# Turning new keys and values into token rows: VectorE 32x32 block transposes and 128 B stores in place of TensorE transposes

## The chip, the cores and the metric

The kernel runs on one core of a Trainium2 chip. The metric is device time in microseconds (us) of one execution. A core has a matrix engine (TensorE; PE in the profile, its weight loads PEld), a vector engine (VectorE, DVE), a scalar engine (ScalarE, ACT), GpSimd (POOL) and a sync engine (SP) that here issues nearly all DMAs. Each engine runs its own instructions in the order in which the program lists them; semaphores join the engines. SBUF is the on-chip memory with 128 partitions, PSUM holds the results of TensorE, DRAM is off-chip.

## The reference, cut to what matters

One inference step of a hybrid layer: 1040 prompt tokens (16 learned meta tokens, then 1024 real ones) and 32 sample tokens (8 requests of 4), all of width 2048. They go through one input projection into eight stick-breaking attention heads of width 128, four gated-linear-attention heads and their gates, and then through one output projection. Besides the layer's result the step returns the new keys and values of the eight heads, as token rows:

```python
def step(...):
    (q, k, v), sg, (gq, gk, gv, gf), gg = branch_inputs(h, w_in[l], w_alpha[l], b_alpha[l])
    o_sb = sb_prompt(q, k, v, sb_bias[l])
    ...
    k_p.append(k)      # (1, 1, 1040, 8, 128) after the stack
    v_p.append(v)
    ...
    k_s.append(k)      # (1, 8, 4, 8, 128)
    v_s.append(v)
```

In `new_k_prompt[0, 0, token, head, :]` the 128 numbers of one token and head are 512 contiguous bytes; the next token of the same head lies 4096 bytes further.

## The kernel before, in words

**Projection.** `inproj` makes one 128-column slice of the input projection for all 1072 tokens, with the result transposed: 128 output columns on the partitions, tokens along the free dimension. Every fp32 operand is split in a high and a low part, so each product is three matmuls (lines 289 to 291). The loop runs over eight weight chunks of 256 rows; in each over three groups of tokens with an accumulator each; in each over two row blocks. That makes 18 matmuls per chunk and 144 per slice. `weight_chunk` loads a chunk (`wr`), ACT casts it (`wh`, line 184) and DVE subtracts (`wl`, line 185). Each of the three tiles has three buffers, and weight work is urgent for the scheduler. After the last chunk `evac` copies each accumulator out.

**Token groups.** `CHUNKS` are 384, 384 and 304 tokens. Values and keys use `SCHUNKS` instead: 378, 378 and 316, which are multiples of `KT` = 126, since the attention's key tiles hold 126 keys and one carry column.

**Heads.** `head(h)` makes the values (`ev_v`), the keys (`ev_k`) and the queries of a head, and then spawns its attention. So PE works through slices V, K, Q of head 0, V, K, Q of head 1 and so on, and the attention of a head is woven into the slices of the next. The table of the profile below gives the three slices of one head.

**What happens to a value or key group.** ACT copies the accumulator to a staging tile `raw` (128 head columns x tokens). `split_k` splits keys into high and low parts in the layout of the key tiles (ACT line 601, DVE line 602). `tok_out` turns the group into token rows: three TensorE transposes (line 457) into one PSUM tile, copies by ACT into a staging tile `st` (lines 459 to 462), and stores on the SP queue of 512 B per token (lines 465 to 468). `load_v` (lines 478, 480) later reads the values back from the output in DRAM, as token rows, for the attention.

**The other work in the same time.** `z_feed` scores the sample queries against the paged key cache on DVE: for each of 512 pages a load of 64 KB (`kp`, line 342) and four multiply-and-accumulate instructions (`jk`, line 384). A page is taken every two beats, a beat being a third of a weight chunk, and loads run six pages ahead. `attend_tile` is a chain PE `z` (505 to 507), DVE 511, ACT 512 and 513, DVE 514, ACT and DVE split (490, 491), PE `z` again (526, 527), ACT 531, split (490, 491), PE `O` (539 to 541). The stages of one tile are set `yield 2`, `D1` = 4 and `D2` = 6 beats apart.

**Order.** The program emits instructions through a `Weaver`, whose generators are continued after a number of beats, and a scheduler then fixes each engine's order when the kernel is built. At run time every engine, and SP's DMA issue, keeps that order.

Of the kernel before, what the change touches and what calls it, by code (L numbers as in the profile page):

```python
# [10 lines left out]
F32 = mybir.dt.float32  # L11
# [71 lines left out]
def hybrid_step(ctx: ExitStack, tc: tile.TileContext, x_prompt, x_sample, cache_k, cache_v, state_gla,  # L83
# [3 lines left out]
    nc = tc.nc  # L87
# [21 lines left out]
    def stage(nm, dt=F32):  # L109
        return stg.tile([P, 384], dt, tag="stg", name=nm)  # L110
# [79 lines left out]
    with tc.tile_pool(name="xp", bufs=2) as xp, tc.tile_pool(name="xps", bufs=5, space=PSUM) as xps:  # L190
# [57 lines left out]
        for c, (lo, hi) in enumerate(CHUNKS):  # L248
            n = hi - lo
            for k in range(NK):  # L250
# [14 lines left out]
                    load_x(5)  # L265
                if (c, k) in NORMS:
                    norm_x(NORMS[c, k])
            lo, hi = SCHUNKS[c]
            o_ = first[c][:, :hi - lo]
            for k in range(NK):  # L270
                wh, wl = (t[:, k % 2, :] for t in wchunks[k // 2])
# [4 lines left out]
                for i in (6, 7, 8):  # L276
                    load_x(i)

    def inproj(c0, evac, lo0, nm, chunks=CHUNKS):

        acc = [accp.tile([P, 512], F32, tag="acc", name=f"acc_{nm}_{c}") for c in range(3)]
        for kk in range(NK // 2):
            wh, wl = weight_chunk(w_in[0], kk, c0, f"{nm}_{kk}")
            for c, (lo, hi) in enumerate(chunks):
                lo = max(lo, lo0)
                n = hi - lo
                for k2 in range(2):
                    k = 2 * kk + k2
                    mm(acc[c][:, :n], wh[:, k2, :], hh[k][:, lo:hi], start=(k == 0), stop=False)  # L289
                    mm(acc[c][:, :n], wh[:, k2, :], hl[k][:, lo:hi], start=False, stop=False)  # L290
# [153 lines left out]
    with tc.tile_pool(name="sp", bufs=1) as sp, tc.tile_pool(name="sps", bufs=1, space=PSUM) as sps:  # L444
# [1 line left out]
        bias0 = sp.tile([P, HEADS], F32, name="bias0")  # L446
        vec.tensor_copy(bias0[:], biasb[:])
        pool.memset(bias0[0:1, :], -1e30)
        def tok_out(raw, c, lo, hi, h, outp, outs_, nm):

            yield 6
            os_ = outs_[0].rearrange("b t h d -> (b t) h d")
            ps = sps.tile([P, 512], F32, tag="z", bufs=4, name=f"tk_{nm}_{c}")
            st = stage(f"st_{nm}_{c}")
            for i in range(3):
                r = min(KT, hi - lo - i * KT)
                nc.tensor.transpose(ps[:r, i * P:(i + 1) * P], raw[:, i * KT:i * KT + r], ident[:])
# [12 lines left out]
        def load_v(h, V):  # L470

# [105 lines left out]
            heads_ready.append(h)  # L577

        def head(h):
            def ev_v(c, ps, lo, hi):  # L580
                raw = stage(f"vraw{h}_{c}")
                act.copy(raw[:, :hi - lo], ps)
                W.spawn(tok_out(raw, c, lo, hi, h, new_v_prompt, new_v_sample, f"v{h}"))
            if h:
                inproj(C_SV + h * P, ev_v, 0, f"v{h}", SCHUNKS)
            else:
                for c, (lo, hi) in enumerate(SCHUNKS):
# [6 lines left out]
            ks = sp.tile([P, NSMP], F32, tag="ks", name=f"ks{h}")  # L594

            def split_k(raw, c, lo, hi):
                for i0, n, w in ((0, 3, KT),) if c < 2 else ((0, 2, KT), (2, 1, 32)):
                    d = [t[:, (3 * c + i0) * P:(3 * c + i0 + n) * P] if w == KT else t[:, 8 * P:KW] for t in kt]
                    d = [t.rearrange("p (a x) -> p a x", a=n)[:, :, 1:w + 1] for t in d]
                    r = raw[:, i0 * KT:i0 * KT + n * w].rearrange("p (a x) -> p a x", a=n)  # L600
                    act.copy(d[0], r)
                    vec.tensor_tensor(d[1], r, d[0].bitcast(F32), ALU.subtract)
# [12 lines left out]
            qsm = sp.tile([P, NSMP], F32, tag="qsm", name=f"qsm{h}")  # L615

# [924 lines left out]
```

## Time and profile before

| | |
|---|---|
| three runs, median (lowest to highest) | 2123.5 us (2121.63 to 2123.98) |
| span of the profiled execution, its own time | 2126.0 us, 2.5 us over the median |
| granted TensorE clock, mean | 0.993 |
| slices V, K, Q of head 2, start to start | 309.4, 339.3, 373.1 and 402.3 us: 29.9, 33.8 and 29.2 us |
| heads' slices on PE | from the first key slice at 73.6 us to the first gate slice at 796.6 us |
| transposes of `tok_out` | from 80.4 us (values of head 0) to 753.9 us (keys of head 7) |

Reading the profile: the page gives each engine's busy time over the span, then 40 slices of the span, then the chain of waits that ends last, then groups of instructions, `out<-in`, with count, busy time and mean duration. The duration of a matmul covers its way through the array, so successive ones overlap, and the time that one adds to PE is better read from start to start. On DVE too the recorded durations of neighbours overlap by some 0.08 us. The windows view gives the busy time of each engine between two moments.

### The profile page before, as it was taken

How to read it: one execution, taken by the hardware profiler on the slowest of the kernel's cores; microseconds unless marked ns; L12 is line 12 of the kernel's file. 1: busy time of each engine (PE TensorE's matmuls, PEld its weight loads, DVE VectorE, ACT ScalarE, POOL GpSimd, SP SyncE). 2: the span in 40 equal slices, each digit the busy share in tenths (PEclk: the TensorE clock that was granted, in tenths of full speed). 3: DMA queues.
4: the chain of work that ended last, by engine and by line, in shares of the span. 5: the costliest groups of instructions: out<-in, count | busy, mean ns of one | idle time of the engine just before them, and what ended most of it. 6: DMA issues, size and time to landing. Idle time of an engine off the chain costs nothing.

```text
span 2126.0 us, 43346 instructions
## 1 busy us (share of the span) xinstructions
PE 2062.8 (97%) x12546; PEld 1872.1 (88%) x12546; DVE 1573.4 (74%) x6592; ACT 995.7 (47%) x2536; POOL 81.8 (4%) x298
## 2 busy tenths in 40 slices
PE   5999999999999999999999999999999999999997
PEld 5999999999999989999898998998888897777765
DVE  6368888889888889898798898978544446453575
ACT  7345556565555646434435335353444335342332
POOL 0000000100001000100000000000000000000000
PEclk9999999999999999999999999999999999999999
DMA  6234443544444354554343444335777665452484
GB/s 198 72 99 127 129 127 103 142 127 113 136 130 121 109 138 118 158 137 116 113 128 109 132 122 128 96 86 151 239 225 241 223 192 185 136 153 75 129 285 171
DMA packets 380442, 304.02 MB, mean 143 GB/s; under 512 B 50410, under 2 KB 320682, under 8 KB 380202
## 3 DMA queue, kind: packets, MB, share of 16 engines
q1 hardware_dynamic: 378010, 300.97, 49.0%
q8 instruction: 99, 1.62, 0.3%
q14 instruction: 141, 1.16, 0.2%
q10 hardware_dynamic: 2192, 0.27, 0.1%
HBM read 243.39 MB, written 57.72 MB: 142 GB/s over the span
## 4 chain that ended last, share of the span: by engine, by line
PE 82%; DVE 7%; DMA 6%; ACT 2%; issue 2%; SPq 0%; POOL 0%; ACTq 0%; DVEq 0%; POOLq 0%
PE acc_g L289 4%; PE acc_g L291 4%; PE acc_g L290 4%; PE b L1450 4%; PE b L1451 4%; PE b L1452 4%; PE acc_k L289 3%; PE acc_k L290 3%; PE acc_k L291 3%; PE acc_q L289 3%; PE acc_q L290 3%; PE acc_q L291 3%; PE acc_v L289 3%; PE acc_gv L289 3%; PE acc_gv L291 3%; PE acc_gv L290 3%
## 5 line engine op out<-in xcount | busy, mean ns | idle before, releaser
L384 DVE SCALAR_TENSOR_TENSOR jk<-kp,qb 128x128 f32<-128x128 f32 x2048 | 591.0, 289 | 39.7 <-DMA qb<-qsd 2.3
L289 PE MATMUL acc_g<-hT,wh_g 128*128 128x368 f32 (+2 forms) x768 | 251.3, 327 | 1.3 <-ACT gx L438 1.2
L291 PE MATMUL acc_g<-hT,wl_g 128*128 128x368 f32 (+2 forms) x768 | 248.0, 323 | 0.0
L290 PE MATMUL acc_g<-hT,wh_g 128*128 128x368 f32 (+2 forms) x768 | 247.6, 322 | 0.0
L1450 PE MATMUL b<-ring,f 128*128 128x512 f32 x416 | 166.7, 402 | 6.6 <-ACT gx L438 3.7
L1314 DVE TENSOR_TENSOR ring<-wr,ring 128x512 fp32r<-128x512 f32 x104 | 70.7, 690 | 134.8 <-ACT ring L1313 134.3
L384 DVE DVE_READ_ACCUMULATOR jk<-kp,qb 128x1 f32 x2048 | 166.4, 81 | 0.0
L1451 PE MATMUL b<-ring,f 128*128 128x512 f32 x416 | 163.5, 393 | 0.8 <-DVE ring L1314 0.7
L1452 PE MATMUL b<-ring,f 128*128 128x512 f32 x416 | 163.2, 392 | 0.0
L289 PEld LDWEIGHTS acc_g<-hT,wh_g 128*128 128x128 f32 x768 | 144.7, 188 | 13.1 <-issue 7.3
L291 PEld LDWEIGHTS acc_g<-hT,wl_g 128*128 128x128 f32 x768 | 144.6, 188 | 2.0 <-issue 2.0
L290 PEld LDWEIGHTS acc_g<-hT,wh_g 128*128 128x128 f32 x768 | 144.7, 188 | 0.7
L1313 ACT CAST ring<-wr 128x512 fp32r<-128x512 f32 x104 | 64.4, 622 | 163.0 <-DMA wr<-in_w_out_dram 72.9
L289 PE MATMUL acc_gv<-hT,wh_gv 128*128 128x384 f32 (+1 forms) x384 | 129.2, 337 | 0.0
L289 PE MATMUL acc_k<-hT,wh_k 128*128 128x378 f32 (+1 forms) x384 | 127.6, 332 | 0.0
L290 PE MATMUL acc_k<-hT,wh_k 128*128 128x378 f32 (+1 forms) x384 | 125.4, 326 | 0.0
L289 PE MATMUL acc_q<-hT,wh_q 128*128 128x368 f32 (+2 forms) x384 | 125.3, 326 | 0.0
L291 PE MATMUL acc_gv<-hT,wl_gv 128*128 128x384 f32 (+1 forms) x384 | 125.3, 326 | 0.0
L291 PE MATMUL acc_k<-hT,wl_k 128*128 128x378 f32 (+1 forms) x384 | 125.2, 326 | 0.0
L290 PE MATMUL acc_gv<-hT,wh_gv 128*128 128x384 f32 (+1 forms) x384 | 124.7, 325 | 0.0
L290 PE MATMUL acc_q<-hT,wh_q 128*128 128x368 f32 (+2 forms) x384 | 123.6, 322 | 0.0
L291 PE MATMUL acc_q<-hT,wl_q 128*128 128x368 f32 (+2 forms) x384 | 123.5, 322 | 0.0
(427 smaller groups left out, 5403.5 us busy)
## 6 DMA issues: line engine op xcount, KB each, us to landing
kp<-in_cache_k_dram SPq DMA_DIRECT2D x512, 64.0 KB
vr<-in_cache_v_dram SPq DMA_DIRECT2D x64, 512.0 KB
tf<-in_w_out_dram SPq DMA_DIRECT2D x64, 256.0 KB
qb<-qsd SPq DMA_DIRECT2D x64, 256.0 KB
td<-tf SPq DMA_DIRECT2D x64, 256.0 KB
wr_g<-in_w_in_dram SPq DMA_DIRECT2D x128, 128.0 KB
wr<-td SPq DMA_DIRECT2D x64, 256.0 KB
wr<-in_w_out_dram SPq DMA_DIRECT2D x48, 256.0 KB
```

The costliest lines, as they stand in the source:

```text
L289: mm(acc[c][:, :n], wh[:, k2, :], hh[k][:, lo:hi], start=(k == 0), stop=False)
L290: mm(acc[c][:, :n], wh[:, k2, :], hl[k][:, lo:hi], start=False, stop=False)
L291: W.mark = mm(acc[c][:, :n], wl[:, k2, :], hh[k][:, lo:hi], start=False, stop=(k == NK - 1)).ins
L384: ins = vec.scalar_tensor_tensor(jk[:], kp[:], 1.0, qbs[h, b][:, t, :], ALU.mult, ALU.mult, accum_out=zt[:, t, NPG - 1 - i:NPG - i])
L1313: act.copy(wh, r)
L1314: vec.tensor_tensor(wl, r, wh.bitcast(F32), ALU.subtract)
L1450: mm(bk[:], ah, wh, start=first and k == 0, stop=False, skip_group_check=True)
L1451: mm(bk[:], ah, wl, start=False, stop=False, skip_group_check=True)
L1452: mm(bk[:], al, wh, start=False, stop=last and k == 7, skip_group_check=True)
```

## The change

`tok_out` no longer uses PE, PSUM or ACT. DVE transposes each 32x32 block of the staged group in place of a full transpose, into one tile `st` of 128 x 1088 for the whole slice (`vst` for values, `kst` for keys; both share one buffer). In that tile, partition 32i + r holds, for every block j, the 32 head columns 32i to 32i + 31 of token 32j + r. After the third group four DMAs, one for each i, store the tokens 0 to 1023 of the head: each moves 32 x 32 runs of 32 numbers, 128 B. The last 16 prompt tokens and the sample tokens have blocks of their own and DMAs of their own; those of the keys' last 16 tokens are kept in `tails` for all heads and stored by `last_keys` after head 7. Since 378 is no multiple of 32, values and keys go back to `CHUNKS`, and `split_k` cuts the groups where the 126-key tiles begin: eight pieces per head where there were four.

```diff
-SCHUNKS = [(0, 3 * KT), (3 * KT, 6 * KT), (6 * KT, T)]
...
-        def tok_out(raw, c, lo, hi, h, outp, outs_, nm):
-            yield 6
-            os_ = outs_[0].rearrange("b t h d -> (b t) h d")
-            ps = sps.tile([P, 512], F32, tag="z", bufs=4, name=f"tk_{nm}_{c}")
-            st = stage(f"st_{nm}_{c}")
-            for i in range(3):
-                r = min(KT, hi - lo - i * KT)
-                nc.tensor.transpose(ps[:r, i * P:(i + 1) * P], raw[:, i * KT:i * KT + r], ident[:])
-            if c < 2:
-                act.copy(st[:KT], ps[:KT, :384])
-            else:
-                act.copy(st[:KT, :256], ps[:KT, :256])
-                act.copy(st[:64, 256:], ps[:64, 256:384])
-            sv = st[:].rearrange("p (a d) -> p a d", d=P)
-            nt = 3 if c < 2 else 2
-            nc.sync.dma_start(outp[0, 0, lo:lo + nt * KT, h, :].rearrange("(a p) d -> p a d", p=KT), sv[:KT, :nt])
-            if c == 2:
-                nc.sync.dma_start(outp[0, 0, 8 * KT:REAL, h, :], sv[:32, 2, :])
-                nc.sync.dma_start(os_[:, h, :], sv[32:64, 2, :])
+        tails = sp.tile([P, HEADS, 32], F32, name="tails")
+        def tok_out(raw, c, lo, hi, h, st, outp, outs_, keep):
+            yield 2
+            w = 384 if c < 2 else 256
+            vec.transpose(st[:, lo:lo + w], raw[:, :w])
             if c < 2:
+                return
+            last = tails[:, h, :] if keep else st[:, SEQ:SEQ + 32]
+            vec.transpose(last, raw[:, SEQ - lo:SEQ + 32 - lo])
+            vec.transpose(st[:, SEQ + 32:], raw[:, REAL - lo:T - lo])
+            yield 1
+            for i in range(4):
+                dst = outp[0, 0, 0:SEQ, h, 32 * i:32 * i + 32].rearrange("(j r) c -> r j c", r=32)
+                nc.sync.dma_start(dst, st[32 * i:32 * i + 32, 0:SEQ].rearrange("r (j c) -> r j c", c=32))
+            if not keep:
+                for i in range(4):
+                    nc.sync.dma_start(outp[0, 0, SEQ:REAL, h, 32 * i:32 * i + 32], st[32 * i:32 * i + META, SEQ:SEQ + 32])
+            a = outs_[0].rearrange("b t h d -> (b t) h d")[:, h, :]
+            nc.sync.dma_start(bass.AP(tensor=a.tensor, offset=a.offset, ap=[[32, 4], [HEADS * P, NSMP], [1, 32]]),
+                              st[:, SEQ + 32:])
+        def last_keys():
+            for i in range(4):
+                nc.sync.dma_start(new_k_prompt[0, 0, SEQ:REAL, :, 32 * i:32 * i + 32], tails[32 * i:32 * i + META])
...
+            vst = sp.tile([P, SEQ + 64], F32, tag="st", name=f"vst{h}")
...
-                inproj(C_SV + h * P, ev_v, 0, f"v{h}", SCHUNKS)
+                inproj(C_SV + h * P, ev_v, 0, f"v{h}")
...
             def split_k(raw, c, lo, hi):
-                for i0, n, w in ((0, 3, KT),) if c < 2 else ((0, 2, KT), (2, 1, 32)):
...
+                t0, e = lo, min(hi, REAL)
+                while t0 < e:
+                    i, x = divmod(t0, KT)
+                    n = (e - t0) // KT if x == 0 else 0
+                    w = KT if n else min(KT - x, e - t0)
+                    n = max(n, 1)
...
                     act.copy(d[0], r)
                     vec.tensor_tensor(d[1], r, d[0].bitcast(F32), ALU.subtract)
+                    t0 += n * w
...
+            kst = sp.tile([P, SEQ + 64], F32, tag="st", name=f"kst{h}")
...
-                W.spawn(tok_out(raw, c, lo, hi, h, new_k_prompt, new_k_sample, f"k{h}"))
-            inproj(C_SK + h * P, ev_k, 0, f"k{h}", SCHUNKS)
+                W.spawn(tok_out(raw, c, lo, hi, h, kst, new_k_prompt, new_k_sample, True))
+                if c == 2 and h == HEADS - 1:
+                    W.spawn(last_keys(), 4)
+            inproj(C_SK + h * P, ev_k, 0, f"k{h}")
```

More of the change, by code (lines that the diff above doesn't have):

```diff
@@ L277, in hybrid_step, with inproj @@
                     load_x(i)
-    def inproj(c0, evac, lo0, nm, chunks=CHUNKS):
+    def inproj(c0, evac, lo0, nm):
         acc = [accp.tile([P, 512], F32, tag="acc", name=f"acc_{nm}_{c}") for c in range(3)]
@@ L283, in inproj @@
             wh, wl = weight_chunk(w_in[0], kk, c0, f"{nm}_{kk}")
-            for c, (lo, hi) in enumerate(chunks):
+            for c, (lo, hi) in enumerate(CHUNKS):
                 lo = max(lo, lo0)
@@ L470, in load_v @@
+        def last_keys():
+            for i in range(4):
+                nc.sync.dma_start(new_k_prompt[0, 0, SEQ:REAL, :, 32 * i:32 * i + 32], tails[32 * i:32 * i + META])
+            return
+            yield
         def load_v(h, V):
@@ L582, in ev_v @@
                 act.copy(raw[:, :hi - lo], ps)
-                W.spawn(tok_out(raw, c, lo, hi, h, new_v_prompt, new_v_sample, f"v{h}"))
+                W.spawn(tok_out(raw, c, lo, hi, h, vst, new_v_prompt, new_v_sample, False))
             if h:
-                inproj(C_SV + h * P, ev_v, 0, f"v{h}", SCHUNKS)
+                inproj(C_SV + h * P, ev_v, 0, f"v{h}")
             else:
-                for c, (lo, hi) in enumerate(SCHUNKS):
+                for c, (lo, hi) in enumerate(CHUNKS):
                     with urgent():
@@ L596, in split_k @@
             def split_k(raw, c, lo, hi):
[L597 to L600 removed]
+                t0, e = lo, min(hi, REAL)
[4 more added lines that the diff above has]
+                    n = max(n, 1)
+                    if n > 1:
+                        d = [t[:, i * P:(i + n) * P].rearrange("p (a x) -> p a x", a=n)[:, :, 1:w + 1] for t in kt]
+                        r = raw[:, t0 - lo:t0 - lo + n * w].rearrange("p (a x) -> p a x", a=n)
+                    else:
+                        d = [t[:, i * P + 1 + x:i * P + 1 + x + w] for t in kt]
+                        r = raw[:, t0 - lo:t0 - lo + w]
                     act.copy(d[0], r)
                     vec.tensor_tensor(d[1], r, d[0].bitcast(F32), ALU.subtract)
+                    t0 += n * w
                 if c == 2:
```

1 line of the change is left out of this document (removed).

## The prediction, made before the result was known

> **What bounds the kernel now.** I read the page's totals and slices first, then the chain of waits, then the windows of one head.
>
> ```profile
> span 2126.0 us, 43346 instructions
> PE 2062.8 (97%) x12546; PEld 1872.1 (88%) x12546; DVE 1573.4 (74%) x6592; ACT 995.7 (47%) x2536; POOL 81.8 (4%) x298
> PE   5999999999999999999999999999999999999997
> DVE  6368888889888889898798898978544446453575
> PE 82%; DVE 7%; DMA 6%; ACT 2%; issue 2%; SPq 0%; POOL 0%; ACTq 0%; DVEq 0%; POOLq 0%
> ```
>
> PE is busy in every slice and makes 82% of the chain that ends last. The DVE row stands at 8 or 9 tenths just where the heads run (slices 3 to 15). So work taken from PE counts there in full, and work given to DVE goes to the engine with the least room. The windows view of head 2 says how little; its lines are the slices V, K and Q.
>
> ```profile
> 309.40:339.30 29.90, 29.90 (x185) 28.63 (x185) 25.76 (x131) 15.41 (x45) 3.15 (x9) 1.00 0.48 136
> 339.30:373.10 33.80, 33.80 (x200) 31.95 (x200) 30.58 (x137) 21.42 (x51) 1.25 (x5) 1.00 0.40 103
> 373.10:402.30 29.20, 29.20 (x184) 28.59 (x183) 24.11 (x119) 16.98 (x44) 3.10 (x13) 1.00 0.58 160
> ```
>
> The columns are length, then busy time of PE, PEld, DVE, ACT and POOL, the granted clock, the DMA share and GB/s. PE has no idle time in 92.9 us. DVE has 29.90 - 25.76 = 4.1 us in V, 3.2 in K and 5.1 in Q. The clock is 1.00, so nothing is to be won there.
>
> **What PE loses.** The first two rows are from PE's timeline and give starts, the last two from the chain of waits.
>
> ```profile
> 160.54 0.49 PE L457 MATMUL tk_v<-ident,vraw 128*126 128x128 f32 x3
> 160.79 0.39 PE L289 MATMUL acc_k<-hT,wh_k 128*128 128x316 f32 x1
> ...
> 344.77 0.33 PE tk_v L457 x3
> 377.99 0.33 PE tk_k L457 x3
> ```
>
> Three transposes take 0.25 us from their start to the next matmul's, and 0.33 us on the chain. There are 16 tensors (values and keys of eight heads) of three such sets: 48 sets, 12.0 to 15.8 us. I take 0.28 us and 13.4 us, 1.7 us per head; none of it is hidden, as PE has no idle time.
>
> The groups become 384, 384, 304 in place of 378, 378, 316, the same 1072 columns. Keys (before) and linear-attention values (already in the other groups) show the price:
>
> ```profile
> L290 PE MATMUL acc_gv<-hT,wh_gv 128*128 128x384 f32 x256 | 86.2, 337 | 0.0
> L290 PE MATMUL acc_k<-hT,wh_k 128*128 128x378 f32 x256 | 86.1, 336 | 0.0
> L290 PE MATMUL acc_k<-hT,wh_k 128*128 128x316 f32 x128 | 39.3, 307 | 0.0
> L290 PE MATMUL acc_gv<-hT,wh_gv 128*128 128x304 f32 x128 | 38.5, 301 | 0.0
> ```
>
> Twice +1 and once -6 ns, 48 times in each of 16 tensors, would be -3 us; that is within the scatter of such means, so I take 0 with 3 us to either side.
>
> **What ACT loses** are four evacuations per tensor, and it gains eight small split pieces in place of four per head. ACT is busy 21.42 of 33.80 us at most, so I count nothing; it can only answer DVE sooner.
>
> **What DVE gains.** No 32x32 transpose stands in the trace. The nearest rows are two-operand passes of the same widths; a one-operand pass bounds them from below.
>
> ```profile
> L429 DVE TENSOR_TENSOR gs<-gs,gx 128x384 f32<-128x384 f32 x16 | 8.8, 552 | 0.0
> L185 DVE TENSOR_TENSOR wl_gv<-wr_gv,wh_gv 128x256 fp32r<-128x256 f32 x64 | 27.0, 422 | 1.5 <-ACT wh_gv L184 1.2
> L602 DVE TENSOR_TENSOR k<-kraw,k 128x32 fp32r<-128x32 f32 x8 | 1.5, 192 | 1.8 <-ACT k L601 1.8
> L236 DVE TENSOR_SCALAR x<-x,r_x 128x1024 f32<-128x1024 f32 x16 | 11.4, 750 | 0.3
> ```
>
> Per tensor: 552 + 552 + 422 + 2 x 192 ns = 1.91 us, 3.8 per head. The lower end is half of it (750 ns for 1024 columns is 281 for 384); the upper end is twice it, should a block have to be filled before it is emptied. I take the middle, since both operations move one fp32 element per column. Four more split pieces per head add at most 4 x 0.16 us (192 ns less the 32 columns). Neighbours overlap, as two rows of DVE's timeline show (start, duration):
>
> ```profile
> 357.71 0.42 DVE L185 TENSOR_TENSOR wl_k<-wr_k,wh_k 128x256 fp32r<-128x256 f32 x1
> 358.05 0.28 DVE L384 SCALAR_TENSOR_TENSOR jk<-kp,qb 128x128 f32<-128x128 f32 x1
> ```
>
> That is 0.08 us, 14 times a head: 3.8 + 0.6 - 1.1 = 3.3 us.
>
> There is a second load. In the built kernel's SP order, the stores of values stand between weight loads, and between two page loads (`kp`) now stand five weight loads and nine stores, where before it was one or two weight loads. DVE's order follows: of 49 `jk` in a V slice, 38 remain in head 4 and 31 in head 5; the others move into K and Q. The row is the K window for `jk` alone:
>
> ```profile
> 339.30:373.10 33.80, 14.74 (x101) 0.00 (x0) 1.00 0.40 103
> ```
>
> 101 instructions are some 50 `jk` with their accumulator reads: 0.29 us each, so 11 to 18 of them are 3.2 to 5.2 us.
>
> K and Q together: DVE 30.58 + 24.11 + 3.3 + 3.2 to 5.2 = 61.2 to 63.2 us, against 63.0 - 1.7 = 61.3 us of PE. To this come DVE's waits in these two windows that PE's lead doesn't cause:
>
> ```profile
> DVE X L514 <- ACT X L513: 2.2, 5, 1.0
> DVE lo_a L491 <- ACT hi_a L490: 1.1, 2, 0.7
> DVE V L484 <- ACT V L483: 1.1, 1, 1.1
> ```
>
> With these 4.4 us DVE is 4.3 to 6.3 us late by the end of Q. V takes that back: 25.76 less 3.2 to 5.2 of 29.9 us.
>
> **What is late next.** A chunk lasts 33.8 / 8 = 4.2 us in K and 3.65 in Q. `wl` is made two chunks ahead (three buffers), 7.3 to 8.4 us, which holds the lag. The attention has six beats, two chunks, between `z` and the split that PE needs, and its own chain takes part of that:
>
> ```profile
> L511 DVE TENSOR_SCALAR X<-z,bias 127x512 f32<-127x512 f32 x48 | 35.8, 746 | 3.4 <-PE z L507 3.3
> L512 ACT ACTIVATE X<-X 127x512 f32<-127x512 f32 x48 | 30.3, 630 | 45.0 <-DVE X L511 44.8
> L513 ACT ACTIVATE X<-X 127x512 f32<-127x512 f32 x48 | 30.1, 628 | 0.3
> L514 DVE SCALAR_TENSOR_TENSOR X<-z,bias,X 127x512 f32<-127x512 f32 x48 | 35.9, 748 | 8.0 <-ACT X L513 8.0
> L490 ACT CAST hi_s<-X 127x512 fp32r<-127x512 f32 x48 | 29.6, 616 | 0.3
> L491 DVE TENSOR_TENSOR lo_s<-X,hi_s 127x512 fp32r<-127x512 f32 x48 | 32.9, 685 | 0.7 <-ACT hi_s L490 0.7
> ```
>
> These sum to 4.05 us, which leaves 3.3 to 4.4 us for a lag of 4.3 to 6.3. Not every tile meets the worst of it, so I take 0.7 us of PE per head in the seven slice triples with attention beside them: 5 us. The bounds are 0 and the rival below.
>
> **Stores, SP and the new waits.** Small packets are in the trace: one load of 2048 runs of 64 B, here with its neighbours in a window of 1.6 us, and its issue on SP with the one behind it.
>
> ```profile
> DMA packets 380442, 304.02 MB, mean 143 GB/s; under 512 B 50410, under 2 KB 320682, under 8 KB 380202
> q1 hardware_dynamic: 378010, 300.97, 49.0%
> ...
> DMA packets 2204, 0.16 MB, mean 97 GB/s; under 512 B 2203, under 2 KB 2203, under 8 KB 2203
> q1 hardware_dynamic: 2203, 0.15, 94.0%
> ...
> 756.93 0.41 SPq L302 DMA_DIRECT2D war<-in_w_in_dram  x1
> 757.43 1.25 SPq L389 DMA_DIRECT2D zd<-zt  x1
> ```
>
> A packet there costs 1.6 us x 16 x 0.94 / 2203 = 11 ns of an engine; over the whole span it is 2126 x 16 x 0.49 / 378010 = 44 ns. A new store of 1024 runs thus takes 0.7 to 2.8 us on the 16 engines, and a tensor's four 2.8 to 11. They are spread over four chunks (15 us) with the queue 40 to 58% busy, so weight loads, issued some three chunks before the cast, stay covered. I count 0. [...]
>
> [...]
>
> `kst` shares its buffer with `vst`, so DVE's first key transpose waits for the value stores; behind it stand `wl` and the attention. SP has the last of these stores ahead of the third query chunk's load, which waits for the split of the last key chunk, and DVE reaches the transpose two chunks (7.3 us) later: hidden, unless a store train takes over 7 us more. `load_v` moves behind the next head's values on SP, and the last `O` of each head keeps its slice in PE's order: nothing.
>
> **Sum.** -13.4 + 0 + 5 = -8.4 us. The profiled span of 2126.0 is 2.5 us over the median of the runs, so it becomes 2117.6, and the median 2123.5 becomes 2115. With no lag and 15.8 + 3 us won it is 2105.
>
> **Rivals.**
>
> - *DVE becomes the bound in K and Q.* At the upper price of the transposes 3.8 us per head come on top, so the lag is 8.1 to 10.1 us, some 5.2 past what the attention holds, in seven triples 37 us: 2123.5 - 13.4 + 37 = 2147. It decides from the point where the lag exceeds 5.7 us (13.4 / 7 paid per head), which is about 0.72 us for a 384-column transpose. For it: 30.58 of 33.80 us busy. Against it: V's idle time refills the lead each head, and waits on ACT shrink when DVE is late. [...]
> - *The small stores hold up the loads.* At 100 ns a packet a store takes 6.4 us, a train 25.6 us where 14.8 are there; past the weights' lead of 8.4 us remain 2.4 us, in 15 trains 36: 2123.5 - 13.4 + 36 = 2146. Against it: 11 and 44 ns above.
> - *The gain is given back.* Lag and longer groups (+3) eat 10 to 17 of the 13.4 us: 2120 to 2127. For it: PE never idles in a head now, and any new wait shows at once.
>
> **How the numbers follow.** Forecast 0.50 (its own range 2105 to 2119), DVE as the bound 0.30, gain given back 0.12, stores 0.08. The measurement tells 0.2%, 4.2 us, from no change. Faster: 0.47 of the forecast's half and 0.01 = 0.48; same: 0.03 + 0.10 = 0.13; slower: 0.30 + 0.08 + 0.01 = 0.39. The range goes from 2106 to 2146 and so takes in most of the slower cases.
>
> **What would show it.** Right: no row for line 457's transposes on PE; PE busy time in the heads unchanged per us but the first gate slice starting some 8 us earlier than 796.6; block transposes of 0.55 us for 384 columns; DVE idle near zero in K and Q, over 6 us in V; waits of PE on `hi_s`, `lo_s` of a few us. Wrong: transposes of 0.8 us and more, PE waiting on DVE for over 15 us in the heads, weight casts waiting for DMA, SP issues of several us at the stores, or heads as long as before.

## The result and the profile after

The changed kernel takes 2199.3 us (median of five runs, 2196.4 to 2200.0) where the kernel before took 2121.6 beside it: ratio 1.0357, 95% interval 1.0346 to 1.0368. It is slower by 3.6%, where a gain had been forecast, and above the predicted range. These lines of its page answer to those of before.

```profile
span 2194.6 us, 42807 instructions
...
PE 2079.6 (95%) x12402; PEld 1872.1 (85%) x12402; DVE 1593.1 (73%) x6704; ACT 983.8 (45%) x2504; POOL 84.1 (4%) x298
...
PE   5999999899989887999999999999999999999997
...
DVE  6477878796878787989889798887644437453475
...
PE 53%; DVE 11%; DMA 8%; ACT 3%; issue 3%; SPq 2%; POOL 0%; DVEq 0%; POOLq 0%; ACTq 0%
```

PE's row has 8s and a 7 where it had only 9s, all in the heads; its share of the chain falls from 82% to 53%. 144 matmuls are gone and PE's busy time has nevertheless grown by 16.8 us. DVE does not look like a new bound: its row is no fuller than before.

The windows view from the first key slice to the first gate slice (length; busy time of PE, PEld, DVE, ACT, POOL; clock; DMA share; GB/s) says what was lost where. First before, then after, then a run shown below in which the four stores are one transfer of 512 B runs (e2).

```profile
73.60:796.60 723.00, 719.96 (x4388) 686.36 (x4386) 594.11 (x2767) 399.39 (x1025) 55.82 (x198) 1.00 0.45 123
```

```profile
73.00:870.20 797.20, 738.10 (x4243) 686.91 (x4242) 613.30 (x2873) 388.42 (x993) 57.41 (x198) 0.96 0.43 110
```

```profile
72.00:776.80 704.80, 701.07 (x4245) 665.79 (x4243) 608.59 (x2879) 383.17 (x993) 56.80 (x198) 1.00 0.46 126
```

The whole loss lies here: the first gate slice starts 73.6 us later than before, and what lies behind it is no longer than before (1324.4 us for 1329.4). Against e2, which has the same instructions on PE, DVE and ACT, the heads are 92.4 us longer. PE stands idle 797.2 - 738.1 = 59.1 us in place of 3.7 (55.4 more), and its 4243 matmuls take 738.1 us in place of 701.1 (37.0 more) at a mean clock of 0.96.

**One stall followed back.** These are rows of the timelines of PE, ACT and SP in a query slice of the changed kernel (start, duration; in brackets the idle time ahead and what ended it).

```profile
606.75 0.33 PE L287 MATMUL acc_q<-hT,wh_q 128*128 128x384 f32 x1
612.09 0.49 PE L545 MATMUL O<-hi_a,V 127*128 127x150 f32 x1 [5.01 <-ACT hi_a L496]
```

```profile
593.66 0.59 ACT L550 COPY ost<-O 128x512 f32<-128x512 f32 x1 [2.09 <-DVE lo_a L497]
...
610.89 0.39 ACT L537 ACTIVATE Y<-z,bias 127x150 f32<-127x150 f32 x1 [4.67 <-DMA od<-ost]
...
611.72 0.32 ACT L496 CAST hi_a<-Y 127x150 fp32r<-127x150 f32 x1 [0.28 <-POOL Y L539]
```

```profile
605.39 0.39 SPq L179 DMA_DIRECT2D wr_q<-in_w_in_dram  x1
606.57 0.34 SPq L340 DMA_DIRECT2D kp<-in_cache_k_dram  x1
606.95 0.43 SPq L403 DMA_DIRECT2D tf<-in_w_out_dram  x1
607.43 0.43 SPq L551 DMA_DIRECT2D od<-ost  x1
```

PE stands 5.01 us for `hi_a`; that waits for `Y`, and `Y` for a buffer that it shares with `ost`, the attention output of another tile. `ost` stood ready at 594.25 us, but SP issued its store at 607.43, 13.2 us later: in the built order fourteen other transfers stand between. Three of them are weight loads that wait for VectorE to free a buffer (0.6, 1.5 and 1.4 us by SP's waits); most of the rest is the time that SP takes to issue them, six page loads with the reads of their page numbers above all (some 1.1 us each on SP's timeline). Over all 16 such stores the time from the end of the copy to the issue has a median of 13.1 us, against 0.5 before.

Where SP itself waits has changed with the order (waits view of SP from 80 to 860 us, before and after; lines 180 and 179 are weight loads, 342 and 340 page loads):

```profile
SPq L342 <- DVE jk L384: 75.3, 116, 2.7
SPq L180 <- DVE jk L384: 69.2, 102, 4.9
```

```profile
SPq L179 <- DVE jk L382: 132.5, 92, 4.6
...
SPq L340 <- DVE jk L382: 6.7, 11, 1.4
```

Summed over all such rows of the heads, SP waits 124 us at weight loads and 88 at page loads before, 248 and 10 after. A page, an output or a re-read that stands behind such a weight load waits along with it. The waits view of 73 to 870 us (total, times, longest) names the other transfers that came late in the same way: pages for the score products, and values read back from DRAM.

```profile
DVE jk L382 <- DMA kp<-in_cache_k_dram: 55.7, 38, 4.4
```

```profile
ACT Y L537 <- DMA od<-ost: 47.7, 11, 8.4
ACT V L489 <- DMA vr<-out_dram: 23.5, 14, 6.2
```

**What a stall costs PE.** The windows view, microsecond by microsecond behind that stall:

```profile
612.38:613.40 1.02, 1.02 (x6) 1.02 (x5) 0.98 (x3) 0.13 (x1) 0.00 (x0) 0.50 0.41 116
...
616.40:617.40 1.00, 1.00 (x5) 1.00 (x4) 0.76 (x5) 0.93 (x3) 0.28 (x1) 0.50 0.00 0
617.40:618.40 1.00, 1.00 (x7) 1.00 (x7) 1.00 (x5) 0.23 (x1) 0.00 (x0) 0.88 0.00 1
```

Behind the 5.01 us of idleness the granted clock stands at 0.50 until 617.6 us, for 5.5 us after PE has resumed. Matmuls of 368 columns start 0.31 us apart in this stretch (from 616.48 us), 0.17 us apart ahead of the stall (from 605.75 us). So this stall is paid once as idle time and again at the lower clock.

The heads of the changed kernel have twelve stretches at 0.50. This is the windows view's sum over them (length; busy time of the engines):

```profile
sum 64.86, PE 50.05 PEld 45.84 DVE 49.71 ACT 27.76 POOL 7.81; mean PE 4.17 PEld 3.82 DVE 4.14 ACT 2.31 POOL 0.65
```

PE starts 168 matmuls in these stretches. At the 701.07 / 4245 = 0.165 us that one adds in e2 they would take 28 us. So some 22 of the 37.0 us are the half clock, by this estimate; the other 15 came at a clock of 1.00, and no run isolates their cause.

**What had been feared.** The group of VectorE's transposes of values (from the view of the tile; minimum, median, maximum in ns), and the DMA view of 201.0 to 204.0 us, in which one key store was issued at 201.05:

```profile
L453 DVE STREAM_TRANSPOSE vst<-vraw x24: 432/570/578, 72.5 to 763.4; 128x384 f32<-128x384 f32 x16, 128x256 f32<-128x256 f32 x8
L457 DVE STREAM_TRANSPOSE vst<-vraw x8: 166/201/209, 74.2 to 764.0; 128x32 f32<-128x32 f32 x8
```

```profile
DMA  0000000012453699999999999988100000000000
...
DMA packets 1313, 0.27 MB, mean 90 GB/s; under 512 B 1056, under 2 KB 1312, under 8 KB 1312
```

A transpose of 384 columns takes 0.57 us, and 1024 runs of 128 B are through within 2.2 us of their issue (by the DMA records they are moved in the last 1.0 us of it). By the updates of the DMAs' semaphores a store of the four lands 2.7 us after its issue (median), a weight load 2.4 before and 2.3 to 2.4 after, a page 2.2 and 2.0. Neither weight loads nor pages have become slower; they are issued late.

### The profile page after: what moved, and what is told of

Its sections match the earlier page's. It is cut to its first block, busy times and chain, and to the rows that moved or that the text cites. A ratio compares the mean times of both kernels' runs of the same rounds, so it can differ in the third digit from the quotient of the medians.

```text
span 2194.6 us, 42807 instructions
## 1 busy us (share of the span) xinstructions
PE 2079.6 (95%) x12402; PEld 1872.1 (85%) x12402; DVE 1593.1 (73%) x6704; ACT 983.8 (45%) x2504; POOL 84.1 (4%) x298
## 4 chain that ended last, share of the span: by engine, by line
PE 53%; DVE 11%; DMA 8%; ACT 3%; issue 3%; SPq 2%; POOL 0%; DVEq 0%; POOLq 0%; ACTq 0%
PE acc_g L287 4%; PE acc_g L289 4%; PE acc_g L288 4%; DVE jk L382 4%; PE b L1471 4%; PE b L1472 4%; PE b L1473 4%; PE acc_gv L287 2%; PE acc_gv L288 2%; PE acc_gv L289 2%; PE acc_gq L289 1%; PE dO L1112 1%; PE acc_gq L288 1%; PE acc_gq L287 1%; DMA kp<-in_cache_k_dram 1%
## 5 line engine op out<-in xcount | busy, mean ns | idle before, releaser
L287 PE MATMUL acc_q<-hT,wh_q 128*128 128x368 f32 (+2 forms) x384 | 127.8, 333 | 1.8 <-ACT kraw L629 1.8
L287 PE MATMUL acc_k<-hT,wh_k 128*128 128x384 f32 (+1 forms) x384 | 126.4, 329 | 0.0
L288 PE MATMUL acc_q<-hT,wh_q 128*128 128x368 f32 (+2 forms) x384 | 126.3, 329 | 0.0
L288 PE MATMUL acc_k<-hT,wh_k 128*128 128x384 f32 (+1 forms) x384 | 124.8, 325 | 0.0
L289 PE MATMUL acc_k<-hT,wl_k 128*128 128x384 f32 (+1 forms) x384 | 124.6, 324 | 0.0
```

## The experiments

All ran beside the kernel before on the same chip. Three theories stood at the start: the *order theory* (SP's built order holds up other transfers), the *DVE theory* (the transposes load VectorE) and the *packet theory* (65,536 runs of 128 B are dear).

### One part taken out: e1, e2, e3, e4

**e1_block** leaves out the transposes but for one block column each, and so most of the transposed data; POOL fills the two tiles with zeros first (`memset`, not shown here):

```diff
-            vec.transpose(st[:, lo:lo + w], raw[:, :w])
+            vec.transpose(st[:, lo:lo + 32], raw[:, :32])
```

> The changed kernel, its stores and their order on SP kept, but each block transpose of 384 or 256 columns cut to its first 32 columns (the rest of the new keys and values is left zero). Order theory (page loads stand on SP behind stores and weight loads, and DVE waits for the pages): the starved page loads stay, 2175 to 2200 us. DVE theory (the transposes overfill VectorE): some 20 us of DVE work are gone, 2105 to 2130 us. Packet theory (128 B runs hold up the loads): 2180 to 2200 us.

Measured: 2202.1 us, ratio 1.0368 (1.0343 to 1.0393). As slow as the change: the DVE theory falls.

**e2_rows** writes the tile in one store of 1024 runs of 512 B; the tokens are misplaced in the output:

```diff
-            for i in range(4):
-                dst = outp[0, 0, 0:SEQ, h, 32 * i:32 * i + 32].rearrange("(j r) c -> r j c", r=32)
-                nc.sync.dma_start(dst, st[32 * i:32 * i + 32, 0:SEQ].rearrange("r (j c) -> r j c", c=32))
+            nc.sync.dma_start(outp[0, 0, 0:SEQ, h, :].rearrange("(a p) d -> p a d", p=P),
+                              st[:, 0:SEQ].rearrange("p (a d) -> p a d", d=P))
```

> The changed kernel with its transposes, but tokens 0 to 1023 of a tensor stored by one DMA of 1024 runs of 512 B (the numbers land in other places than the reference's). Order theory: one short store in place of four, page loads keep their places on SP, 2105 to 2120 us. DVE theory: 2180 to 2200 us. Packet theory: 2105 to 2120 us.

Measured: 2105.0 us, ratio 0.9909 (0.9892 to 0.9925). The same bytes and the same work on PE, DVE and ACT: the gain that was predicted is there, and at 19 us more than twice as large.

**e3_idle** gives the four stores the lowest priority (`with idle():`).

> The changed kernel, all of its work, with the four stores given the lowest priority for the scheduler, so that page loads go ahead of them on SP. Order theory: 2105 to 2125 us. DVE theory: 2180 to 2200 us. Packet theory: 2180 to 2200 us, as the same 65,536 runs are stored.

Measured: 2139.7 us, ratio 1.0068 (1.0051 to 1.0085): most of the loss gone, some 15 us more than expected.

**e4_act** issues the four stores from ACT (`nc.scalar.dma_start`).

> The changed kernel, all of its work, with the four stores issued on ACT's DMA queue, so that SP's order is nearly that of before. Order theory: 2105 to 2130 us, unless ACT is held by the issue. DVE theory and packet theory: 2180 to 2200 us.

Measured: 2122.4 us, ratio 0.9987 (0.9976 to 0.9998). All 65,536 small runs and all transposes are in it: the packet theory falls too, as the cause of this loss. A key slice takes 33.9 us in it, 32.5 in e2: ACT, with the stores in its own queue, comes later to the attention (from 80 to 870 us PEld waits 10.9 us for `hi_a`, a wait that does not appear in e2).

### Guesses at one late thing: e5, e6, e9, e10, e12 to e15

**e5_lead9** asks for pages eight ahead, with nine buffers (`bufs=9`, `n + 8`).

> The changed kernel with pages of the cache asked for eight ahead in place of six (nine page buffers in place of seven); stores, transposes and the built order around the stores stay as they are (five weight loads still stand between two page loads seven times, as against eight). If what costs is that VectorE comes to a page that has not been loaded (page-lead theory), five weight loads are some 7.5 pages of VectorE's work: a lead of eight covers it, the waits of jk for kp (56.9 us in the changed kernel) fall under 10 us and the time comes to 2105-2135. If what costs is the stores' own occupancy of the DMA queue or the changed order of PE and ACT, nothing changes: 2190-2205.

Measured: 2195.6 us, ratio 1.0327 (1.0303 to 1.0351).

**e6_spread3** puts `yield 3` behind each of the four stores.

> The changed kernel with three beats between the four stores of a tensor (about one weight chunk), nothing left out. In the built order there are then almost always at most two weight loads between two page loads. Order theory: the time comes to what the 512 B stores gave, 2100-2115, since the same bytes in the same packets are only spread. Store-cost theory (the 17 us between the two kernels with moved and with replaced stores are the price of 65,536 small packets): 2118-2130. If spreading leaves the page loads late in some heads: 2130-2160 with jk still waiting for kp.

Measured: 2180.7 us, ratio 1.0255 (1.0232 to 1.0278). Neither the page-lead theory of e5 nor any of the ranges for e6 held. Counting weight loads between two page loads was the wrong measure: it does not tell whether a load stands behind a weight load that itself waits for VectorE. SP's waits in the heads do: 249 us at weight loads and 7 at page loads in e5, 238 and 8 in e6, which is the changed kernel's 248 and 10 over again.

**e9_pagefirst** gives page loads the weight loads' priority.

```diff
-            with tc.issue_after(done[-4]):
+            with urgent(), tc.issue_after(done[-4]):
                 pg = load()
-        d = nc.sync.dma_start(dst, ...)
+        with urgent():
+            d = nc.sync.dma_start(dst, ...)
```

> The changed kernel with the page loads (and the reads of their page numbers) at the priority of the weight loads; stores, transposes and everything else as in the changed kernel, on SP's queue. Counted in the built order, in estimated time of VectorE's instructions: between the last buffer release that SP has waited for ahead of a page load and the product that needs the page lie 10.7 us in the median and under 4 us for 41 of 384 pages in the changed kernel; 15.8 us and none in the kernel before; here 16.0 us and none, because 7 page loads in place of 247 stand behind a weight load that waits for its buffer. In the run with a longer lead it was 11.7 and 28, in that with spread stores 10.9 and 48, and both stayed slow. Order theory (in this form: a page load stands on SP behind a weight load whose buffer VectorE frees late): the waits of jk for kp fall from 56.9 to under 10 us and the time to 2110-2150, the rest being re-reads of values and stores that still stand behind weight loads. Store-cost theory: 2180 or more.

Measured: 2253.1 us, ratio 1.0626 (1.0595 to 1.0657): worse. The waits for `kp` are gone, and these stand in their place (80 to 890 us, waits of DVE and of ACT):

```profile
DVE jk L383 <- DMA qb<-qsd: 33.5, 13, 4.4
...
DVE kst L454 <- DMA out_dram<-vst: 14.8, 6, 3.2
```

```profile
ACT Y L538 <- DMA od<-ost: 46.9, 11, 7.2
```

**e10_loadsfirst** puts the re-reads of values and the stores of attention outputs there too (`with urgent():` around both).

> As the run before, with the re-reads of values and the stores of attention outputs at that priority too. Order theory: the waits of ACT for vr (23.5 us in the changed kernel) and of Y for od<-ost (47.7 us) go as well; 5 to 30 us below the run with the page loads alone, down to 2100-2115. If these stand ahead of weight loads that are then late in turn (13 of 242 weight loads have under 4 us, as against 11): 2120-2150.

Measured: 2222.0 us, ratio 1.0464 (1.0446 to 1.0483): 31 us below e9, and still above every time that was expected. The attention outputs now leave 1.1 us after their copy (median), but the loads of the scores' queries (31.8 us of VectorE's waits) and of the low-rank weights (17.7 us of PE's) are late. Each kind of transfer that was moved forward moved the hold-up to another.

**e12_lead3**: the kernel before with three page buffers and pages asked for two ahead (`bufs=3`, `n + 2`).

> The kernel before with three page buffers in place of seven and pages asked for two ahead in place of six; nothing else is changed, and nothing of the change is in it. In the built order a page then has 6.8 us in the median (24 of 384 under 4 us) between the release SP waits for and its use, as late as in the changed kernel. If late pages alone make the loss: jk waits for kp by 30 us and more, and the time is 2150-2200. If they need the stores beside them: 2122-2135.

Measured: 2158.5 us, ratio 1.0158 (1.0138 to 1.0178), at the low end of what late pages alone were expected to do; `jk` waits 27.8 us for `kp`. But only 8.0 us of the longer span lie in the heads (731.0 us for 723.0), and 27.5 lie behind them, where the changed kernel lost nothing. So late pages cost time by themselves, without the change, and in the heads about a ninth of the 73.6 us.

**e13_shift**: the kernel before with the score products paced so that they crowd into key slices.

```diff
-        W.spawn(z_feed(lambda n: 2), lasting=True)
+        def rate(n):
+            s = (W.now + 36) % 72 // 24
+            return (3, 1, 2)[s] + (n % 5 < (0, 3, 0)[s]) - (n % 3 == 0 and s == 0)
+        W.spawn(z_feed(rate), lasting=True)
```

> The kernel before; only the pace of the page products is changed, so that in VectorE's built order 57 to 63 of them stand in a key slice, 41 to 45 in a query slice and 38 to 42 in a value slice (before 50, 48 and 46; the changed kernel 42 to 59, 39 to 50 and 36 to 54). No transfer and no other work differs, and pages have their lead (10.3 us for all but the worst twentieth). Displaced-order theory: VectorE has some 37 us of work in a key slice of 33.8, comes 3 us late, less the 3 to 4 us that the attention holds: 2130-2190, PE waiting for hi_s, lo_s, hi_a. If the order of VectorE has slack and the late loads are what costs: 2120-2130.

Measured: 2121.2 us, ratio 0.9981 (0.9971 to 0.9990): 57 to 63 products in a key slice cost nothing there, without the transposes.

**e14_pinned** evens out VectorE's order, 48 products in every slice, by an ordering without data:

```diff
-            vec.tensor_tensor(wl, raw[:], wh.bitcast(F32), ALU.subtract)
+            ins = vec.tensor_tensor(wl, raw[:], wh.bitcast(F32), ALU.subtract)
+            if len(jks) > 2 and nm[0] in "vkq":
+                tc.add_manual_dep(ins.ins, jks[-3].name, NOSYNC, reason="pin")
...
+            jks.append(ins.ins)
```

> The changed kernel with one ordering added that moves no data: the second cast of each weight chunk of the heads may not stand ahead of the page product three before it in program order. VectorE's built order then has 48 products in every slice; loads and stores stand on SP as late as in the changed kernel (page to use 11.2 us in the median, 37 of 384 under 4 us; there 10.7 and 41). Displaced-order theory: most of the loss is gone, 2105-2140. Late-load theory: jk waits for kp by 40 us or more as before and the time stays at 2170-2230. Both together: between.

Measured: 2195.8 us, ratio 1.0336 (1.0319 to 1.0353): how the products are spread over VectorE's order is not it.

**e15_pinned_pages** is e14 with e9's edit.

> As the run before, with the page loads at the weight loads' priority too: VectorE's order has 48 products a slice, and pages have 16.5 us to their use (none under 4). Both-together theory: 2105-2135. If it is over 2160, neither is the cause and what is left is the stores' and re-reads' own place on SP (values' re-reads and attention outputs behind weight loads) or PE's and ACT's built order.

Measured: 2249.1 us, ratio 1.0584 (1.0567 to 1.0602). So mending late pages, the spread of the products, or both does not bring the time back.

### Parts by themselves: e7, e8

**e7_groups**: the kernel before with groups of 384, 384, 304 (`CHUNKS` for `SCHUNKS`), TensorE transposes in blocks of 128 tokens, and the new `split_k`.

> The kernel before with the column groups 384, 384, 304 and the eight split pieces alone; TensorE still transposes, in blocks of 128 tokens, and the stores have rows of 512 B in the same number. Its order of page and weight loads is that of before. The prediction counted this part as 0 with 3 us to either side: 2119-2127 beside a kernel before of 2122-2126. If part of the 1.3 us that a key slice gained comes from the groups and not from the transposes, up to 8 us faster: 2115-2119. If the extra split pieces weigh on ACT or VectorE: 2128-2140.

Measured: 2120.5 us, ratio 0.9979 (0.9966 to 0.9991). The first gate slice starts 5.0 us earlier (791.6 us); key and value slices are each 0.3 us shorter.

**e8_quarters**: the kernel before with its stores cut in four.

```diff
-            nc.sync.dma_start(outp[0, 0, lo:lo + nt * KT, h, :].rearrange("(a p) d -> p a d", p=KT), sv[:KT, :nt])
+            for i in range(4):
+                cs = slice(32 * i, 32 * i + 32)
+                nc.sync.dma_start(outp[0, 0, lo:lo + nt * KT, h, cs].rearrange("(a p) d -> p a d", p=KT), sv[:KT, :nt, cs])
```

> The kernel before with each store of tokens cut into four stores of 128 B runs, TensorE transposes and groups as before: 48 sets of four stores in place of 48 stores, the small packets of the change without its transposes. In the built order up to three weight loads stand between two page loads (15 and 5 times two and three). Order theory: such gaps are within the lead of six pages, so at most a few us: 2120-2132. Store-cost theory: 17 us or more over the kernel before, 2138-2150.

Measured: 2151.2 us, ratio 1.0116 (1.0094 to 1.0138), just over what the store-cost theory had put down, though VectorE's built order has the same products in every slice as before, and the stores land in 2.0 us (median). What is late shows in ACT's waits (80 to 870 us):

```profile
ACT V L485 <- DMA vr<-out_dram: 38.4, 16, 6.3
```

These were 7.2 us before. The values' re-read reads what the stores write, and with 144 more stores on SP it comes later.

### The order crossed with the stores: e17, e18

If four stores with runs of 512 B stand in the place of the four with 128 B, the same count of instructions, the scheduler builds another order. So the two can be crossed: each kernel's instructions are held on every engine to the order that was built for the other.

```diff
+        traced = {i.name: i for i in nc.cur_bb.bb.instructions}
+        for names in (order or {}).values():
+            names = [n for n in names if n in traced]
+            for a, b in zip(names, names[1:]):
+                tc.add_manual_dep(traced[b], a, NOSYNC, reason="order")
```

**e17_order**: the stores of the change, in the order built for 512 B (the lines show the ordering alone; a first build with the 512 B stores supplies the names).

> The changed kernel, all its work and its 128 B stores on SP's queue, with the order of the instructions on every engine fixed to the one that the scheduler builds when each of the four stores has runs of 512 B (1024 of them in all; 4096 of 128 B as run here). VectorE then has 50, 48 and 46 products a slice and a page 15.3 us to its use. Order theory (the scheduler's order is the whole cause, the packets cost little): 2100-2118, at or below the run with the stores on ACT. Run-time theory (the small stores do something on SP's queue): 2160 or more. Between: both.

Measured: 2125.3 us, ratio 1.0001 (0.9989 to 1.0012): 7 us above the order theory's range, 35 below the other's.

**e18_crossed**: four stores of 512 B runs (tokens and columns misplaced in the output), in the order of the changed kernel.

> The other corner: the four stores of a tensor have runs of 512 B (256 each; rows of four features sets are misplaced in the output), and the order of the instructions on every engine is fixed to the one of the changed kernel. Order theory: as slow as the changed kernel, 2180-2205, with the waits of jk for kp and of Y for od<-ost. Run-time theory: 2100-2130.

Measured: 2213.9 us, ratio 1.0411 (1.0386 to 1.0436), 9 us above the order theory's range. Its windows line and its waits from 73 to 880 us are the changed kernel's over again:

```profile
72.80:875.10 802.30, 738.41 (x4244) 686.97 (x4242) 613.63 (x2873) 387.70 (x993) 57.47 (x198) 0.96 0.41 110
```

```profile
DVE jk L383 <- DMA kp<-in_cache_k_dram: 57.7, 40, 4.3
ACT Y L543 <- DMA od<-ost: 53.1, 12, 8.6
...
ACT V L495 <- DMA vr<-out_dram: 23.4, 13, 4.8
```

The same stores in the other order (e17): the attention outputs leave after 1.4 us, and of these three waits the re-read is left, beside 3.5 us for `od` (73 to 800 us, waits of ACT).

```profile
73.60:792.70 719.10, 705.93 (x4244) 666.05 (x4243) 608.92 (x2879) 384.11 (x993) 57.60 (x198) 1.00 0.49 123
```

```profile
ACT V L495 <- DMA vr<-out_dram: 23.8, 11, 4.7
```

This is the answer: with the order goes the time, whichever stores stand in it. Compared by tiles and shapes in the traces, e18 has the changed kernel's order on every engine, instruction by instruction. That of e17 differs from it on every engine and not on SP alone: of PE's 12402 matmuls 12038 stand in the same order, of ACT's 2504 instructions 2124, of VectorE's 6704 5476. So what is shown is the built order as a whole; that SP's part of it carries the loss is argued from the waits.

The table sets the main runs side by side. Page products per key slice are counted in VectorE's order; SP's waits in the heads, at weight loads and at page loads, and the median time from an attention output's copy to the issue of its store are from the traces.

| kernel | products in a key slice | SP's waits at weight loads and at page loads, us | output waits on SP, us | ratio |
|---|---|---|---|---|
| before | 50 | 124, 88 | 0.5 | 1 |
| after | 42 to 59 | 248, 10 | 13.1 | 1.0357 |
| e2, one store of 512 B | 50 | 116, 85 | 0.1 | 0.9909 |
| e9, pages first | 43 to 57 | 94, 223 | 13.5 | 1.0626 |
| e13, products crowded, no change | 57 to 63 | 128, 95 | 0.1 | 0.9981 |
| e14, products evened out | 48 | 215, 14 | 3.6 | 1.0336 |
| e17, 128 B in the order for 512 B | 50 | 144, 50 | 1.4 | 1.0001 |
| e18, 512 B in the order for 128 B | 42 to 59 | 248, 9 | 13.3 | 1.0411 |

### A version that beats both: e11, e16

**e11_actlate**: the four stores on ACT, `yield 4` ahead of them and `yield 1` between.

> The changed kernel with the four stores issued by ACT, as in the run with stores moved (ratio 0.9987), but the first four beats after the transposes and the others one beat apart, so that ACT does not stand at a store whose transposes VectorE has not done. If the 17 us between the moved and the replaced stores were ACT's standing there (PE waited for hi_a 10.9 us, ACT for stores' semaphores some 17): 2100-2112, a key slice 32.5 us in place of 33.9. If they are the price of the issues or of the packets: 2117-2124 as then.

Measured: 2117.3 us, ratio 0.9966 (0.9954 to 0.9979). Better than e4, but a key slice still has some 33.6 to 34.5 us for e2's 32.5, so spacing the issues did not shorten it; what else 64 stores on ACT cost is not isolated.

**e16_mix**: as e11 for the values, while the keys' stores stay on SP at the lowest priority.

```diff
+                with (idle() if keep else contextlib.nullcontext()):
+                    (nc.sync if keep else nc.scalar).dma_start(dst, ...)
+                yield 1
```

> The changed kernel with the values' four stores issued by ACT (four beats after the transposes, one beat apart) and the keys' four by SP at the lowest priority; nothing left out. It has VectorE's order of 50, 47, 47 products and 15.7 us of page lead. Half the issues on ACT of e11 (2117.3): 2108-2116. If the keys' stores on SP cost as in e3: 2118-2135.

Measured: 2116.3 us, ratio 0.9960 (0.9945 to 0.9974). With nothing left out both are faster than the kernel before, by 7 to 9 us, which is what the prediction hoped of the change as it stands.

## Why the prediction was wrong

**What PE loses** was right. In e2 the first gate slice starts at 776.8 us, 19.8 earlier than before. 5.0 of that are the groups, by e7; predicted were 0 with 3 to either side, so this term was too small. The other 14.8 are the transposes; predicted were 13.4, bounds 12.0 to 15.8.

**What DVE gains** was right in its durations (0.57 us for 0.55), and its consequence was not. (Its turning point of 0.72 us does not follow from its own lag: from the middle, 5.3 us, to 5.7 are 0.4 us of 3.8, a tenth more per transpose, 0.61 us.) A lag of 4.3 to 6.3 us was to cost PE 5 us. In e2, with all the transposes, PE idles 3.7 us in the heads for 3.0 before; and without the transposes the change stays as slow (e1). The *second load*, the products that move into key and query slices, showed no cost: in e13 as many in key slices cost nothing.

**The stores** were right as to the chip: 1024 runs are moved in some 1.0 us, within the 0.7 to 2.8 predicted, and weight loads (2.3 to 2.4 us for 2.4) and pages (2.0 for 2.2) land no later in the median. The rival of small stores that hold up loads had the right victims and the wrong cause: loads are held up, but by their place in the order, with runs of 512 B as with 128 (e18, 1.0411).

**The step that failed** is the sentence "In the built kernel's SP order, ... between two page loads (`kp`) now stand five weight loads and nine stores, where before it was one or two weight loads. DVE's order follows". The signal had been read, and was turned into a count of moved products, 3.2 to 5.2 us of VectorE's work. What it meant is that the built order had changed as a whole, and in it SP's queue: weight loads that wait for VectorE (248 us in the heads for 124) stand ahead of transfers that ACT and VectorE wait for. The section on stores then took weight loads' lead as what had to be covered ("stay covered", "hidden", "nothing"), put no price on pages and attention outputs behind SP's waits, and set the re-read of values, `load_v`, at nothing. In the sum this order stands as part of the 5 us of lag and as 0 for stores, SP and the new waits. No run shows the 0 for SP: of the issue of 1.25 us printed there (757.43 us) 1.1 are a wait for VectorE (`SPq L389 <- DVE jk L384`), and transfers behind SP's waits for VectorE are what came late. The runs showed for it, between ratios of 1.0001 (e17) and 1.0357, 0.0356 x 2121.6 = 76 us.

**A term that was missing**: the prediction said of the clock that "nothing is to be won there". Something was to be lost: some 22 of the 92.4 us, by the estimate above, are PE running at half clock after its stalls. Priced by idle time alone, the loss comes out at 55.4 of 92.4 us.

**The sum** in the runs' terms: -19.8 (e2) + 55.4 idle + 37.0 longer matmuls (some 22 of them the clock) = +72.6. The first gate slice is 73.6 us late; the missing 1.0 us lies ahead of the heads, where the first key slice starts at 73.0 us for e2's 72.0.

**What stays open.** Why the scheduler orders the rest otherwise for runs of 128 B is in no trace; shown is only that the form of the four stores alone, with the same count, does it. Which engine's order carries the loss is not isolated, as e17 and e18 hold all of them at once; the stall followed back and SP's waits speak for SP's. The loss isn't divided among single transfers, since each that was moved forward made others late. Four stores of 512 B in their own order, the last corner of the cross, were not run. And the 20 us between e17 and e2, four stores for one on SP, are put down to late re-reads by the waits of e17 and e8 (23.8 and 38.4 us for 9.6 in e2 and 7.2 before); no run isolates that.

## What to carry to other kernels

Where one in-order queue issues every transfer, compare its built order before and after a change, and ask of each transfer what it stands behind and whether that waits for an engine; the four stores here, at 1.0001 in one order (e17), came with another order of everything else, at 1.0357. When the order changes as a whole, a fix for the one wait that the profile shows on top can move the hold-up elsewhere, as in e9 (1.0626) and e10 (1.0464): put the new transfers on another queue (0.9966 in e11), or hold the rest to the order that worked (e17). And price a PE stall at its length plus what the clock, where it falls, loses after it: here 55.4 us of idle time brought, by estimate, some 22 us at half clock.

## What the runs showed of the hardware that was not expected

A much shorter stall than that of 5.01 us was followed by a lower clock too: one of 1.85 us (190.73 to 192.58 us in the changed kernel) by 3.41 us at 0.50.

```profile
192.60:193.60 1.00, 0.91 (x4) 0.71 (x5) 0.93 (x7) 1.00 (x6) 0.00 (x0) 1.00 0.13 22
...
194.60:195.60 1.00, 1.00 (x5) 1.00 (x4) 1.00 (x5) 0.00 (x0) 0.00 (x0) 0.50 0.35 53
...
196.60:197.60 1.00, 1.00 (x6) 1.00 (x6) 1.00 (x7) 0.66 (x2) 0.74 (x1) 0.50 0.00 0
```

The drop comes 1.8 us after PE has resumed, at 194.38 us; at the stall of 5.01 us it came 1.3 us before PE resumed, at 610.81 us. A stall of 1.60 us (397.41 to 399.01) left the clock at 1.00.

The length of a stall did not decide it alone. One of 1.98 us left the clock at 1.00:

```profile
714.01 0.34 PE L545 MATMUL O<-hi_a,V 127*128 127x150 f32 x1 [1.98 <-ACT hi_a L496]
...
715.00:716.00 1.00, 1.00 (x7) 1.00 (x8) 1.00 (x5) 0.64 (x2) 0.02 (x1) 1.00 0.19 54
```

In the clock record of the trace the twelve stretches at 0.50 in the heads last 3.41 us or a multiple of it, and they start on one grid: the first three in the heads at 194.38, 218.28 and 317.26 us, 7 and 29 times 3.413 us apart. The 1.98 us lie across a line of this grid (713.21 us). How much idle time in one interval brings the drop does not come out: 1.07 us (in 761.00 to 764.41 us) were followed by one and 1.60 us (in 395.77 to 399.18 us) were not.

In the one order in which both were run, 65,536 runs of 128 B took no more time than the same bytes in runs of 512 B (ratios 1.0357 and 1.0411). They did keep the 16 engines busier: a DMA share of 0.49 in e17 against 0.46 in e2, 352 us of 719.1 against 324 of 704.8.
